# A 180-degree image rotation: 64 KB rows in one resident SBUF tile, with the first 16 images on partitions 32 to 95

## The chip, the cores and the metric

The kernel runs on one core of one Trainium2 chip. The time is device time in microseconds (us), the median of several executions. The profile is one execution; its span, from the first to the last instruction, is about 1.5 to 1.8 us shorter than the time. KB and MB of a transfer are powers of two in the text (4 MB is 4,194,304 bytes); GB/s is 10^9 bytes per second.

The five engines meet here as follows: VectorE (DVE in the profile) reverses data inside SBUF; the queues of SyncE (SPq) and ScalarE (ACTq) only issue DMA transfers. The transfers run on the core's 16 DMA engines, which both queues share (in the kernel before, the packets of the one queue took 48.9% of 16 engines' span and those of the other 48.0%).

## The reference

```python
def setup_inputs():
    batch, c, h, w = 32, 3, 256, 256
    return {"x": np.random.randn(batch, c, h, w).astype(np.float32)}

def reference(x):
    return np.rot90(x, k=2, axes=(-2, -1)).astype(np.float32)
```

A rotation by 180 degrees reverses each of the 96 images (32 x 3) of 65,536 floats (256 KB) end to end. So 25.17 million bytes are read, reversed, and 25.17 million written: 50.33 million bytes through the DMA engines.

## The kernel before

Three passes of 32 images. An image is cut into 8 rows of 32 KB; rows 0 to 3 of 32 images fill the 128 partitions of one tile, rows 7 to 4 those of another. VectorE reverses halves of a row, and each half goes out in rows of 16 KB. Two input buffers per tag and four output buffers let the queues run ahead.

```python
    for pp in range(n_pass):                     # 3 passes of NG = 32 images; Q = 4, S = 8
        nsl = slice(pp * NG, (pp + 1) * NG)
        tinF = tin_pool.tile([P, BLK], x.dtype, tag="F")      # 128 x 8192, bufs=2
        tinB = tin_pool.tile([P, BLK], x.dtype, tag="B")
        nc.sync.dma_start(out=tinF[:, :], in_=x3[nsl, 0:Q, :])
        nc.sync.dma_start(out=tinB[:, :], in_=x3[nsl, S - 1:Q - 1:-1, :])

        tF0 = tout_pool.tile([P, HB], x.dtype, tag="t")       # 128 x 4096, bufs=4
        nc.vector.tensor_copy(out=tF0[:, :], in_=tinB[:, 2 * HB - 1:HB - 1:-1])
        nc.scalar.dma_start(out=o4[nsl, 0:Q, 0, :], in_=tF0[:, :])
        # ... three more copies and stores of this form
```

## Time and profile before

| | before |
|---|---|
| time, median | 123.8 us |
| span of the profile | 122.3 us |
| VectorE busy | 27.2 us, 22% |
| data rate over the span | 412 GB/s |
| packets | 2592, of which 2304 carry data |

The page of the kernel before, cut to its main lines. The digits cut the span into 40 slices of 3.06 us; 9 means 90% busy or more. The two last lines are the DMA queues: packets, megabytes, and the share of 16 engines' span that their packets took.

```profile
span 122.3 us, 93 instructions
...
DVE  0000000399500000610160003307337156100000
...
DMA  5798989899999998999999999999999999999992
GB/s 171 343 472 386 472 386 482 375 482 359 348 450 407 466 429 386 472 423 397 439 455 413 477 434 391 413 429 434 429 434 434 439 429 434 429 439 434 429 429 113
DMA packets 2592, 50.33 MB, mean 412 GB/s; under 512 B 288, under 2 KB 288, under 8 KB 288
...
q1 hardware_dynamic: 864, 25.17, 48.9%
q10 hardware_dynamic: 1728, 25.17, 48.0%
```

VectorE idles most of the time while the DMA row has no hole between its ends, and the two queues together hold the 16 engines for 96.9% of the span. This kernel is bound by the DMA engines. Waits of VectorE cost nothing here, since transfers are always queued ahead: the DMA digits are 8 or 9 from the third slice to the last but one.

Rates by stretch, from the windows view of the same kernel (start:end, length, VectorE busy, GpSimd busy, clock, DMA share, GB/s):

```profile
core 0: us, DVE busy (x) POOL busy (x), PEclk, DMA share, GB/s
2.00:25.00 23.00, 1.65 (x1) 0.00 (x0) 1.00 1.02 429
27.00:33.00 6.00, 5.25 (x3) 0.00 (x0) 1.00 1.08 401
33.00:78.00 45.00, 6.88 (x3) 0.00 (x0) 1.00 0.99 427
78.00:120.00 42.00, 11.47 (x5) 0.00 (x0) 1.00 1.01 431
```

The rate is about 430 GB/s whether the engines only read (2 to 25, 429), mix (33 to 78, 427) or only write (78 to 120, 431). Only the stretch where the first stores come in is lower (27 to 33, 401).

The trace also records every packet; a row of a transfer is one packet (768 packets of 32 KB read, 1536 of 16 KB written). A 32 KB read packet takes 1213 ns at the median, a 16 KB write packet 611 ns.

### The profile page before, as it was taken

What the parts mean: (1) busy time and instruction counts of PE and PEld (TensorE: products, weight loads), DVE (VectorE), ACT (ScalarE), POOL (GpSimd) and SP (SyncE); (2) the same over time, 40 slices, a digit from 0 to 9 for tenths busy, and PEclk for the clock granted to TensorE, in tenths of its full rate; (3) what the DMA queues carried; (4) which work ended last, traced back from release to release, by engine and by line L of the source; (5) the groups of instructions that cost most, each with busy time, mean ns of one, the idle gap of its engine ahead of it and who ended that gap; (6) DMA issues with size and microseconds to landing.
All of it is one profiled execution on the core that took longest, in us unless ns stands there. A gap on an engine that the chain in (4) does not pass through costs nothing.

```text
span 122.3 us, 93 instructions
## 1 busy us (share of the span) xinstructions
DVE 27.2 (22%) x12; POOL 0.2 (0%) x4
## 2 busy tenths in 40 slices
DVE  0000000399500000610160003307337156100000
POOL 0000000000000000000000000000000000000000
DMA  5798989899999998999999999999999999999992
GB/s 171 343 472 386 472 386 482 375 482 359 348 450 407 466 429 386 472 423 397 439 455 413 477 434 391 413 429 434 429 434 434 439 429 434 429 439 434 429 429 113
DMA packets 2592, 50.33 MB, mean 412 GB/s; under 512 B 288, under 2 KB 288, under 8 KB 288
## 3 DMA queue, kind: packets, MB, share of 16 engines
q1 hardware_dynamic: 864, 25.17, 48.9%
q10 hardware_dynamic: 1728, 25.17, 48.0%
HBM read 25.17 MB, written 25.17 MB: 412 GB/s over the span
## 4 chain that ended last, share of the span: by engine, by line
DMA 69%; DVE 11%; another core or an unknown queue 4%; SPq 0%; issue 0%; DVEq 0%
DMA out_dram<-tF 37%; DMA tinB<-in_x_dram 18%; DMA out_dram<-tB 14%; DVE tB L64 4%; DVE tF L60 4%; DVE tF L52 2%; DVE tB L56 2%; SPq L48 0%; DVEq L64 0%; DVEq L60 0%
## 5 line engine op out<-in xcount | busy, mean ns | idle before, releaser
L52 DVE COPY tF<-tinB 128x4096 f32<-128x4096 f32 x3 | 6.9, 2294 | 43.8 <-DMA tinB<-in_x_dram 41.2
L60 DVE COPY tF<-tinB 128x4096 f32<-128x4096 f32 x3 | 6.9, 2291 | 14.7 <-DMA out_dram<-tF 14.7
L56 DVE COPY tB<-tinF 128x4096 f32<-128x4096 f32 x3 | 6.9, 2292 | 11.1 <-DMA out_dram<-tB 11.1
L64 DVE COPY tB<-tinF 128x4096 f32<-128x4096 f32 x3 | 6.9, 2291 | 7.6 <-DMA out_dram<-tB 7.6
L80 POOL MEMSET const-bfloat16-1.0<- 128x1 bf16 x1 | 0.1, 102 | 0.0
L80 POOL MEMSET const-uint8-127<- 128x1 uint8 x1 | 0.1, 102 | 0.0
L80 POOL MEMSET const-float32-0.0<- 128x1 f32 x1 | 0.1, 99 | 0.2 <-issue 0.2
L80 POOL MEMSET const-float32-1.0<- 128x1 f32 x1 | 0.1, 99 | 0.0
## 6 DMA issues: line engine op xcount, KB each, us to landing
tinF<-in_x_dram SPq DMA_DIRECT2D x3, 4096.0 KB, 32.2
tinB<-in_x_dram SPq DMA_DIRECT2D x3, 4096.0 KB, 32.9
out_dram<-tF ACTq DMA_DIRECT2D x6, 2048.0 KB, 20.0
out_dram<-tB ACTq DMA_DIRECT2D x6, 2048.0 KB, 23.1
```

Source lines behind the costliest of these rows:

```text
L52: nc.vector.tensor_copy(out=tF0[:, :], in_=tinB[:, 2 * HB - 1:HB - 1:-1])
L56: nc.vector.tensor_copy(out=tB0[:, :], in_=tinF[:, 2 * HB - 1:HB - 1:-1])
L60: nc.vector.tensor_copy(out=tF1[:, :], in_=tinB[:, HB - 1::-1])
L64: nc.vector.tensor_copy(out=tB1[:, :], in_=tinF[:, HB - 1::-1])
L80: nc = _bacc.Bacc("TRN2", target_bir_lowering=False, num_devices=1)
```

## The change

Its intent: fewer and larger packets (rows of 64 and 32 KB), one tile of three 64 KB slots per partition instead of many buffers, and a small first group of 16 images so that stores can start early. Those 16 images take 64 partitions, 32 to 95, filled by four transfers that each take every fourth partition. After that come two groups of 32 images on all 128 partitions and a last group of 16 images, which fills 128 partitions with half-size rows (8 rows of 32 KB per image).

```diff
-    NG = 32
-    ... 3 passes of 32 images, tiles of 32 KB in, 16 KB out
+    E = L // 4                      # 16384 floats: rows of 64 KB
+    K = E // 4                      # 4096: one copy
+    A0, B0, C0 = 0, E, 2 * E        # three slots
+    S = pool.tile([P, 3 * E], x.dtype, tag="S")
+
+    for q in range(4):
+        nc.sync.dma_start(out=S[32 + q:96:4, A0:A0 + E],
+                          in_=rows(xi, 0, 16, 4)[:, q, :])
+    nc.sync.dma_start(out=S[:, B0:B0 + E], in_=rows(xi, 16, 32, 4))
+    for p0 in (32, 64):
+        reverse(C0, A0, E, p0, p0 + 32)                  # 4 copies each
+    nc.scalar.dma_start(out=rows(oi, 0, 16, 4)[:, ::-1, :],
+                        in_=S[32:96, C0:C0 + E])         # first store
+
+    nc.sync.dma_start(out=S[:, A0:A0 + E], in_=rows(xi, 48, 32, 4))   # third load
+    reverse(C0, B0, E)
+    nc.scalar.dma_start(out=rows(oi, 16, 32, 4)[:, ::-1, :],
+                        in_=S[:, C0:C0 + E])             # second store
+
+    nc.sync.dma_start(out=S[:, B0:B0 + E // 2], in_=rows(xi, 80, 16, 8))   # fourth load
+    h = E // 2
+    o = rows(oi, 48, 32, 4)[:, ::-1, :]
+    reverse(B0 + h, A0 + h, h)
+    nc.scalar.dma_start(out=o[:, :, 0:h], in_=S[:, B0 + h:B0 + E])
+    reverse(C0, A0, h)
+    nc.scalar.dma_start(out=o[:, :, h:E], in_=S[:, C0:C0 + h])
+    reverse(A0 + h, B0, h)
+    nc.scalar.dma_start(out=rows(oi, 80, 16, 8)[:, ::-1, :],
+                        in_=S[:, A0 + h:A0 + E])         # last store, 16 x 8 rows
```

Here `rows(t, first, n, s)` views images `first` to `first+n-1` of `t` as `n` images of `s` rows, and `reverse(dst, src, size)` is `size/4096` copies on VectorE.

More of the change, by code (lines that the diff above doesn't have):

```diff
@@ L23 @@
     B, C, H, W = x.shape
-    N = B * C
     L = H * W
-    NG = 32
-    Q = P // NG
-    S = 2 * Q
-    BLK = L // S
-    HB = BLK // 2
-    x3 = x.rearrange("b c h w -> (b c) (h w)").rearrange(
-        "n (s e) -> n s e", s=S)
-    o4 = out.rearrange("b c h w -> (b c) (h w)").rearrange(
-        "n (s j f) -> n s j f", s=S, f=HB)
-    tin_pool = ctx.enter_context(tc.tile_pool(name="tin", bufs=2))
-    tout_pool = ctx.enter_context(tc.tile_pool(name="tout", bufs=4))
-    n_pass = N // NG
-    for pp in range(n_pass):
-        nsl = slice(pp * NG, (pp + 1) * NG)
-        tinF = tin_pool.tile([P, BLK], x.dtype, tag="F")
-        tinB = tin_pool.tile([P, BLK], x.dtype, tag="B")
-        nc.sync.dma_start(out=tinF[:, :], in_=x3[nsl, 0:Q, :])
-        nc.sync.dma_start(out=tinB[:, :], in_=x3[nsl, S - 1:Q - 1:-1, :])
-        tF0 = tout_pool.tile([P, HB], x.dtype, tag="t")
-        nc.vector.tensor_copy(out=tF0[:, :], in_=tinB[:, 2 * HB - 1:HB - 1:-1])
-        nc.scalar.dma_start(out=o4[nsl, 0:Q, 0, :], in_=tF0[:, :])
-        tB0 = tout_pool.tile([P, HB], x.dtype, tag="t")
-        nc.vector.tensor_copy(out=tB0[:, :], in_=tinF[:, 2 * HB - 1:HB - 1:-1])
-        nc.scalar.dma_start(out=o4[nsl, S - 1:Q - 1:-1, 0, :], in_=tB0[:, :])
-        tF1 = tout_pool.tile([P, HB], x.dtype, tag="t")
-        nc.vector.tensor_copy(out=tF1[:, :], in_=tinB[:, HB - 1::-1])
-        nc.scalar.dma_start(out=o4[nsl, 0:Q, 1, :], in_=tF1[:, :])
-        tB1 = tout_pool.tile([P, HB], x.dtype, tag="t")
-        nc.vector.tensor_copy(out=tB1[:, :], in_=tinF[:, HB - 1::-1])
-        nc.scalar.dma_start(out=o4[nsl, S - 1:Q - 1:-1, 1, :], in_=tB1[:, :])
@@ new lines, with rows, reverse @@
+    xi = x.rearrange("b c h w -> (b c) (h w)")
+    oi = out.rearrange("b c h w -> (b c) (h w)")
+    E = L // 4
+    K = E // 4
+    A0, B0, C0 = 0, E, 2 * E
+    pool = ctx.enter_context(tc.tile_pool(name="slots", bufs=1))
+    S = pool.tile([P, 3 * E], x.dtype, tag="S")
+    def rows(t, first, n, s):
+        return t[first:first + n, :].rearrange("n (s e) -> n s e", s=s)
+    def reverse(dst, src, size, p0=0, p1=P):
+        for c in range(0, size, K):
+            hi = src + size - c
+            lo = hi - K
+            nc.vector.tensor_copy(
+                out=S[p0:p1, dst + c:dst + c + K],
+                in_=S[p0:p1, hi - 1:(lo - 1 if lo else None):-1])
```

## The prediction

What is left of the layout step, 4 MB in 9.7 us, is the author's estimate: 4,194,304 bytes at the 433 GB/s of the undisturbed packets in the trace of the kernel before. The 2:1 sharing that step 2 speaks of can be counted in the same trace: from 34 to 78 us 384 read packets of 32 KB and 395 write packets of 16 KB start.

> **What bounds the kernel now.** The 16 DMA engines: the page's slices show DMA at 98-99% nearly throughout, its two queues 96.9% of 16 engines' span; DVE is 22% busy. Packet records: a 32 KB read takes 1211 ns undisturbed, a 16 KB write 611 ns, 48 and 96 per engine: 116.8 us, about 433 GB/s. [...] The rest of the 122.3 us span: first packet at 2.1, slow reads 1.6 (the first of each engine, and from 27 to 33 us as the first writes come in), 0.6 spread between engines, 1.2 from last packet to end. The measured time is 1.45 us above the span.
>
> **What the change does.**
> - *Bytes:* the same 50.33 MB.
> - *Packets:* 611 and 1211 ns imply 11 ns per packet beside the bytes. With 64 and 32 KB rows there are 20 + 8 reads and 12 + 24 writes per engine; at an estimated 2411 ns per 64 KB, 115.9 us. Gain 0.9 us.
> - *Layout:* partitions 32 to 95. [...] I expect full rate: 4 MB in 9.7 us.
> - *DVE:* 2.2 us per 4096-element copy whatever the partitions (assumed), so the first 16 images cost eight copies, 17.7 us. In total 18 copies, 40 us, still far under the DMA, but with three slots instead of six buffers they sit between transfers.
>
> **Where it lands** (433 GB/s, 2.2 us per copy, 0.4 us last packet to landing, 1.4 us issue to first packet, as at the start):
> 1. The first 4 MB lands at 13.3; eight copies end at 31.1; the second load (8 MB) leaves the engines at 31.8. The first write and the third load are issued only at 31.1, first packets 32.5: **gap 1, 0.7 us**.
> 2. They share the engines packet by packet (before: read and write shared 2:1, the ratio of packet sizes). The write ends after about 8 of 12 packet times; landing and spread 1.4, four copies 8.9, issue 1.5: 11.8 us against 9.7 us of reads left: **gap 2, 2.1 us**; none if the write goes first, 4.5 if the reads get one 64 KB packet ahead. Mean 1.8.
> 3. From there 24 MB are queued ahead of DVE; no gap.
>
> Sum: 2.1 + 115.9 + 1.6 + 0.6 + 1.2 = 121.4; with 2.5 of gaps 123.9 span, 125.3 time. The change looks tuned, so I shade down: **125.0 us**, range 122.6 to 127.4. Chances: faster by over 2% 0.06, within 2% 0.70, slower by over 2% 0.24.
>
> **What would show it.** DMA by slices: two dips, near 32 and 63 us, 98-99% elsewhere; about 1200 packets instead of 2592. Groups: 32-partition copies at 2.2-2.3 us each. Waits: DVE waiting about 20 us for the first write (31 to 53) and over 20 us for the second. Chain: first load, eight copies, first write, four copies, then DMA to the end. The last 58 us without a gap.
>
> **What would make it wrong.** Slower: reads running ahead of the first write in 64 KB packets; the strided or 64-partition transfers below 433 GB/s; a more ragged end between engines with large packets. Faster: the slow packets at the first writes vanish; copies of 32 partitions cheaper; shorter issue latency, closing both gaps (121.4 + 1.45 = 122.9).

## The result, and the profile after

The time rose from 123.8 to 140.87 us (four runs, 140.33 to 141.4), a ratio of 1.1383 (95% interval 1.1353 to 1.1413). Executions over 1.5% slower than the fastest of the same kernel are left out of the means. The ratios in this document are not quite the ratios of the medians. The output is right. The predicted 125.0 us and its range (122.6 to 127.4) were missed by far.

The page of the changed kernel, the same lines as before:

```profile
span 139.1 us, 86 instructions
...
DVE  0001999990000000089990000002993000000000
...
DMA  8697996968997896960298999996999999979981
GB/s 301 301 584 320 509 396 301 603 301 301 301 565 339 358 546 301 603 301 0 66 349 339 452 452 452 452 452 301 452 443 452 405 443 396 424 151 301 226 188 38
DMA packets 1216, 50.33 MB, mean 362 GB/s; under 512 B 192, under 2 KB 192, under 8 KB 192
...
q10 hardware_dynamic: 656, 25.17, 47.4%
q1 hardware_dynamic: 560, 25.17, 44.6%
```

There are two things to see. The DMA row has a hole (digits 0 and 2, near 66 us), which the kernel before nowhere has. And at the right end the DMA row is still full, but the GB/s row falls to about half. Busy engines that move half the bytes: that is a different loss from a hole, and the DMA share alone would not have shown it. (GB/s of single slices jump, because a packet is counted whole where it starts. The windows view counts in the same way.)

The windows view of the changed kernel puts numbers on it:

```profile
core 0: us, DVE busy (x) POOL busy (x), PEclk, DMA share, GB/s
2.00:31.00 29.00, 17.49 (x8) 0.00 (x0) 1.00 1.02 434
32.30:39.00 6.70, 0.00 (x0) 0.00 (x0) 1.00 0.99 323
39.00:63.00 24.00, 3.42 (x2) 0.00 (x0) 1.00 1.00 431
63.00:69.00 6.00, 6.00 (x4) 0.00 (x0) 1.00 0.00 0
69.50:77.00 7.50, 3.38 (x2) 0.00 (x0) 1.00 0.97 336
77.00:119.00 42.00, 8.99 (x4) 0.00 (x0) 1.00 1.01 436
119.00:137.00 18.00, 0.00 (x0) 0.00 (x0) 1.00 0.97 233
```

From 63 to 69 us no packet starts. The last packets before the hole end between 63.0 and 63.95, and the next start at 69.5, so an engine idles for 6.2 us on average. From 119 to 137 us the last store of 4 MB runs at 233 GB/s. The two stretches where loads and stores begin together (32 to 39 and 69.5 to 77) run at 323 and 336.

The timeline of the changed kernel (start, length, engine, line, what):

```profile
13.50 17.79 DVE L49 COPY S<-S 32x4096 f32<-32x4096 f32 x8 [13.50 <-DMA S<-in_x_dram]
31.32 0.33 SPq L67 DMA_DIRECT2D S<-in_x_dram  x1
31.32 0.66 ACTq L63 DMA_DIRECT2D out_dram<-S  x1
59.58 13.30 DVE L49 COPY S<-S 128x4096 f32<-128x4096 f32 x6 [28.28 <-DMA out_dram<-S]
68.50 0.33 SPq L73 DMA_DIRECT2D S<-in_x_dram  x1
68.51 0.59 ACTq L69 DMA_DIRECT2D out_dram<-S  x1
...
106.35 1.09 ACTq L83 DMA_DIRECT2D out_dram<-S  x1
```

The third load (L67) and the first store (L63) are issued at the same moment, 31.32. VectorE can go on only when that store has left slot C, at 59.58: 28.3 us for 4 MB. Its next copies end at 68.5, and only then are the next load (L73) and store (L69) issued. The third load had left the engines before 64.

The packet records, worked out per engine (sum over all packets of the time above the shortest packet of that kind and size, divided by 16) give the whole difference:

| us of an engine's time | before | after | difference |
|---|---|---|---|
| packets, undisturbed | 116.8 | 116.2 | -0.6 |
| slow packets of loads | 1.6 | 4.0 | +2.4 |
| slow packets of the last store | 0 | 7.8 | +7.8 |
| idle in the middle (near 32, 66 and 69 us) | 0 | 7.1 | +7.1 |
| start, uneven end, last landing | 3.9 | 4.0 | +0.1 |
| span | 122.3 | 139.1 | +16.8 |

(116.2 is 20 x 2.418 + 8 x 1.213 of reads and 12 x 2.418 + 24 x 1.213 of writes. The idle time was added up from the start and end of every packet. The fifth line is what is left of the span.)

### The profile page after: what moved, and what is told of

It is laid out like the page before. It is cut to its first block, busy times and chain, and to the rows that moved or that the text cites. A ratio compares the mean times of both kernels' runs of the same rounds, so it can differ in the third digit from the quotient of the medians.

```text
span 139.1 us, 86 instructions
## 1 busy us (share of the span) xinstructions
DVE 40.1 (29%) x18; POOL 0.2 (0%) x4
## 4 chain that ended last, share of the span: by engine, by line
DMA 51%; DVE 19%; issue 2%; DVEq 2%; SPq 1%
DMA out_dram<-S 44%; DVE S L49 19%; DMA S<-in_x_dram 8%; DVEq L110 2%; SPq L55 1%; DVEq L49 0%
## 5 line engine op out<-in xcount | busy, mean ns | idle before, releaser
L49 DVE COPY S<-S 128x4096 f32<-128x4096 f32 (+1 forms) x18 | 40.1, 2284 | 65.6 <-DMA S<-in_x_dram 37.0
```

The lines of the kernel that those rows point to most:

```text
L49: nc.vector.tensor_copy(out=S[p0:p1, dst + c:dst + c + K], in_=S[p0:p1, hi - 1:(lo - 1 if lo else None):-1])
```

## The experiments

The theories. **A**: the last store's shape, 16 images of 8 rows, decides which SBUF partitions are read at the same time, and some sets of partitions can be read or written at about half the rate only. This was conjecture: the trace names neither the engine nor the partition of a packet, so experiments 2 and 9 choose the partitions by hand. Rival **B**: the place of the last store, or its HBM addresses (16 images at a pitch of 256 KB), is slow. **C**: the hole comes from 64 KB load packets that run ahead of the first store and then share one to one with it. (In the changed kernel 32 load packets, two per engine on average, start between the first store's issue at 31.32 us and its first packet at 38.86; from 40 to 54 us 48 load packets and 47 store packets start.) Rivals **D** and **E**: it is only the length of the copies and the issue latencies, or a fixed wait of a store.

The first lot of experiments ran against 123.77 us of the kernel before (7 runs), the second against 123.63 (11 runs).

### 1. The same store addressed as 32 blocks of 4 rows

```diff
-    nc.scalar.dma_start(out=rows(oi, 80, 16, 8)[:, ::-1, :], ...
+    w = oi[80:96, :].rearrange("n (a s e) -> (n a) s e", a=2, s=4)
+    nc.scalar.dma_start(out=w[:, ::-1, :], in_=S[:, A0 + h:A0 + E])
```

> Wrong result on purpose: the last 4 MB store writes the same rows of SBUF into the same 4 MB of the output, addressed as 32 blocks of 4 rows instead of 16 images of 8 rows. Theory A [...]: its 32 KB packets fall from about 2.4 us to 1.21 us, the last store from 18.6 us to about 9.7, time 132 us (131 to 133.5). Rival B (the slowness belongs to the last store's place, its source columns or its region of HBM, not to the shape): no change, 140 to 141.5 us.

Measured: 132.65 us (132.24 to 133.19), ratio to before 1.0721. The packets of the last 4 MB fell from a median of 2438 ns to 1213 ns, none slower; from first to last packet they took 10.4 us instead of 18.6. The windows line of this kernel for its last store:

```profile
118.50:128.50 10.00, 0.00 (x0) 0.00 (x0) 1.00 0.97 419
```

So 8.2 us of the loss hang on the shape of the address alone: same bytes, same SBUF source, same 4 MB of HBM. Rival B falls as far as it speaks of place, columns or region. It could still be the order in which single engines touch HBM, if the shape changes that too (the trace does not show it); experiment 9 settles it.

### 2. The first 16 images on partitions 0 to 63

```diff
-        nc.sync.dma_start(out=S[32 + q:96:4, A0:A0 + E], ...
+        nc.sync.dma_start(out=S[q:64:4, A0:A0 + E], ...
-    for p0 in (32, 64):
+    for p0 in (0, 32):
-                        in_=S[32:96, C0:C0 + E])
+                        in_=S[0:64, C0:C0 + E])
```

> First 16 images on partitions 0 to 63 instead of 32 to 95; every HBM address, size, engine count and copy count stays. Theory A [...]: the 64 KB packets of the first four loads take about 4.9 us instead of 2.42, the first load lands near 23 us instead of 13.4, the first store is slowed too; time 150 to 162 us. Rival B (HBM addresses or pitch decide the packet time): packets stay at 2.42 us, time 140 to 141.5 us.

Measured: 153.06 us (152.59 to 153.72), ratio 1.2371. The first 64 load packets took 5082 ns at the median instead of 2418, and the first copy starts 10.4 us later than in the changed kernel (23.88 against 13.50). Windows line and timeline line of this kernel:

```profile
2.00:22.50 20.50, 0.00 (x0) 0.00 (x0) 1.00 1.07 237
...
23.88 17.79 DVE L49 COPY S<-S 32x4096 f32<-32x4096 f32 x8 [23.88 <-DMA S<-in_x_dram]
```

With HBM addresses unchanged, the partitions alone nearly halve the rate: 237 GB/s, where the changed kernel's four loads on partitions 32 to 95 take 2418 ns per 64 KB packet, or 434 GB/s on 16 engines. The engines are as busy as there (DMA share 1.07; in the changed kernel 1.02 from 2 to 31 us). So the choice of 32 to 95 in the change was right. Why partitions 0 to 63 are slow is not shown. One part of the expectation missed: the first store, now read from partitions 0 to 63, was not slowed (its 64 KB packets: 2418 ns at the median). It was issued together with the third load (41.71 and 41.70 us), while no store ran beside the slow loads; whether that spared it was not tested.

### 3. The third load behind the first store, on the same queue

```diff
-    nc.sync.dma_start(out=S[:, A0:A0 + E], in_=rows(xi, 48, 32, 4))
+    nc.scalar.dma_start(out=S[:, A0:A0 + E], in_=rows(xi, 48, 32, 4))
```

> The third load is issued on the store queue, behind the first store. Theory C (gap of 6.2 us near 66 us comes from two 64 KB read packets per engine running ahead of the first store, and then sharing one to one with it): first store packet about 1.2 us after its issue instead of 7.5, store lands near 44 us instead of 59.5, next issue near 52.5 while the third load still runs, no idle stretch in the middle; time 133 to 135.5 us. Rival D (the gap is the copies and issue latencies alone, which the order does not change): 139.5 to 141.5 us.

Measured: 133.25 us (133.21 to 133.42), ratio 1.0771. The first store's packets begin at 32.50, 1.3 us after its issue, instead of at 38.86, and the hole is gone. Windows line of this kernel where the changed one has its hole, then its timeline:

```profile
63.00:69.00 6.00, 1.88 (x1) 0.00 (x0) 1.00 1.01 350
...
31.17 0.67 ACTq L63 DMA_DIRECT2D out_dram<-S  x1
32.02 0.45 ACTq L67 DMA_DIRECT2D S<-in_x_dram  x1
43.80 8.90 DVE L49 COPY S<-S 128x4096 f32<-128x4096 f32 x4 [12.66 <-DMA out_dram<-S]
52.72 0.33 SPq L73 DMA_DIRECT2D S<-in_x_dram  x1
```

The copies still take 8.9 us, and the issues what they were (0.33 us on SPq and 0.59 on ACTq for the pair after these copies, in both kernels). Only the queue of the third load, and with it the order, changed: the store now goes ahead of the load, and slot C is free 11.3 us after the store's first packet instead of 20.7. VectorE gets slot C at 43.80 instead of 59.58, so the next transfers are queued while the third load still runs. Rival D falls.

### 4. The third load as two transfers of 32 KB half rows

```diff
-    nc.sync.dma_start(out=S[:, A0:A0 + E], in_=rows(xi, 48, 32, 4))
+    r3 = rows(xi, 48, 32, 4)
+    for c in (0, E // 2):
+        nc.sync.dma_start(out=S[:, A0 + c:A0 + c + E // 2],
+                          in_=r3[:, :, c:c + E // 2])
```

> The third load as two transfers of 32 KB half rows, on its own queue as before. Theory C: what runs ahead is two packets, so half the bytes, and the packet shares turn to 2:1 for the store: first store packet 3.5 to 4.5 us after issue instead of 7.5, store lands at 50 to 52 us instead of 59.5, gap near 66 us falls from 6.2 us to under 1; time 134 to 136 us. If a fixed wait of the store after an idle queue is the cause (rival E), the first store packet stays near 7.5 us and more than half of the gap remains: 137 us or more.

Measured: three runs took 136.24, 134.31 and 134.68 us, ratio 1.0914 (1.084 to 1.0988); a fourth, 142.03, was slow. The hole fell from 6.2 us of engine idleness to 0.1. VectorE got slot C at 52.92 instead of 59.58. (The slot was expected at 50 to 52.) A line of its timeline:

```profile
52.92 8.90 DVE L49 COPY S<-S 128x4096 f32<-128x4096 f32 x4 [21.82 <-DMA out_dram<-S]
```

But the first store packet came 6.3 us after its issue, not 3.5 to 4.5, and so nearer to rival E's 7.5. Between the issue and it, 48 load packets started, three per engine on average (in the changed kernel 32, two per engine), and these took 1.81 us each on average instead of 1.21. So "two packets run ahead" is not a rule; of 32 KB packets it was three, and they were slow. What helped was mostly the sharing of 64 KB to 32 KB per turn in favour of the store (that they take turns is the reading of the 48 load packets and 47 store packets counted above for the changed kernel): its packets took 13.8 us from first to last instead of 17.8, and the start gave 1.2. Rival E, a wait that every store has, falls by experiment 3, where the store began 1.3 us after its issue. What sets the length of the wait beside a load stays open: other stores waited 5.9 us (the second of the changed kernel, issued together with its fourth load) and 4.1 us (the first of the kernel before, issued while loads ran).

### 5. The kernel before with the packet sizes of the change

```diff
-        tinF, tinB: two loads of 4 MB, rows of 32 KB
+        tin = tin_pool.tile([P, BLK], x.dtype, tag="F")          # BLK = 16384, bufs=2
+        nc.sync.dma_start(out=tin[:, :], in_=x3[nsl, :, :])      # x3 with s=4
-        four stores per pass, rows of 16 KB, tout bufs=4
+        two stores per pass, rows of 32 KB (two copies each), tout bufs=2
```

> The kernel before with the packet sizes of the change alone: loads of 8 MB in rows of 64 KB into two buffers, stores in rows of 32 KB from two buffers, all transfers over 128 partitions with 32x4 stores. Theory: large packets are worth only their fixed cost, 24 x 2.418 + 48 x 1.213 = 116.3 us per engine against 116.8, and queued work leaves no gap: 122.8 to 124.0 us, within 1% of before. Rival (64 KB packets are harmful in themselves, through uneven engines or long slow phases when reads and writes meet): 125 us or more.

Measured: 123.26 us (122.68 to 123.38, 6 runs), ratio 0.9961 (0.9945 to 0.9977), with the right result. Large packets did no harm here, and they are worth 0.4%. This is the one version that beats both kernels, by an amount below 2%.

### 6. Experiments 1 and 3 together

> Both single repairs together (last store as 32 blocks of 4 rows, wrong result on purpose; third load behind the first store). If shape and order are separate causes they add: 140.9 - 8.2 - 7.6 = 125.1 us (124.3 to 126), and no idle stretch and no slow store remain. If one hides the other, 127 us or more.

Measured: 124.97 us (124.8 to 125.01), ratio 1.0107. The single gains are 8.2 and 7.6 us; 140.87 less both is 125.0. The engines' idle time in the middle is 0.6 us, without a hole near 66, and no packet of the last store took over 1213 ns. In the GB/s row of this kernel's page single slices jump, as above, but none falls to zero in the middle, and the end no longer runs at half:

```profile
GB/s 341 341 341 341 682 341 341 618 405 341 341 341 682 277 405 341 341 682 213 469 426 256 448 405 511 511 511 341 341 416 437 426 426 437 416 480 394 490 394 117
```

The two causes are separate and add up, and together they account for all but 1.3 us of the loss (124.97 against 123.63).

### 7. The reversal of the last 16 images' rows moved onto the load

```diff
-    nc.sync.dma_start(out=S[:, B0:B0 + E // 2], in_=rows(xi, 80, 16, 8))
+    nc.sync.dma_start(out=S[:, B0:B0 + E // 2], in_=rows(xi, 80, 16, 8)[:, ::-1, :])
-    nc.scalar.dma_start(out=rows(oi, 80, 16, 8)[:, ::-1, :],
+    nc.scalar.dma_start(out=rows(oi, 80, 16, 8),
```

> Right result: the order of the 8 rows of each of the last 16 images is reversed by the load, so the load has the 16x8 shape and the last store is 128 plain rows. Theory A [...]: last store back to 1.21 us per packet and about 9.7 us; the load's 32 KB read packets slow down instead, by an amount that is open, since its packets alternate with a store's: total 132 to 141 us. Rival B (place, columns or HBM region of the last store): the last store stays at 18.6 us and the load is unchanged, 140 to 141.5 us.

Measured: 139.49 us (138.07 to 140.05), ratio 1.1263, result right. The last store is a plain list of 128 rows now and back at 1213 ns per packet at the median. The fourth load had 1213 ns at the median in the changed kernel: it, too, is written `rows(..., 16, 8)` there, but without the reversal its rows follow one another through all 16 images, which makes it such a plain list. Reversed, it has 1982 ns. (Its packets share the engines with a store's: in the changed kernel 48 of this load's and 64 of the second store's start from 78 to 90 us.) Its completions on the 16 engines also spread over 4.2 us (from 100.9 to 105.1 us) instead of 0.9. The slowness moved with the shape, from a store to a load, and little was won. With this 16x8 shape, where the reversal is written decided which transfer paid, not whether one paid.

### 8. Both causes repaired, with the right result

The third load goes behind the first store as in experiment 3. The second store is cut in two halves, so that its slot is freed earlier. The last 16 images are held like the first 16:

```diff
-    nc.sync.dma_start(out=S[:, B0:B0 + E // 2], in_=rows(xi, 80, 16, 8))
+    for q in range(4):
+        nc.sync.dma_start(out=S[32 + q:96:4, B0:B0 + E],
+                          in_=rows(xi, 80, 16, 4)[:, q, :])
...
+    o3 = rows(oi, 80, 16, 4)[:, ::-1, :]
+    nc.scalar.dma_start(out=o3[:, :, 0:h], in_=S[32:96, A0 + h:A0 + E])
...
+    nc.scalar.dma_start(out=o3[:, :, h:E], in_=S[32:96, A0:A0 + h])
```

> Right result, both causes repaired: third load behind the first store; the last 16 images on partitions 32 to 95 in 64 KB rows like the first 16, stored as 16x4 in two halves; the second store in two halves so that its slot comes free earlier. Theories A and C: no store packet over 1.3 times its undisturbed time, no idle stretch over 1 us in the middle; 2.1 + 115.9 + 2.5 slow packets + 0.7 gap + 1.9 tail = 123.1 us span, 124.6 us time (123 to 126), that is level with before, since the change has only packet overhead to win. A result above 128 us would say that a third cause is left.

Measured: 124.88 us (124.79 to 125.08), ratio 1.0101 (1.0088 to 1.0114). The page of this kernel:

```profile
span 123.1 us, 99 instructions
...
DVE 53.6 (44%) x24; POOL 0.2 (0%) x4
...
DMA packets 1360, 50.33 MB, mean 409 GB/s; under 512 B 272, under 2 KB 272, under 8 KB 272
```

VectorE works twice as long as before (53.6 against 27.2 us) at little cost, since the DMA engines have no long hole. Slow packets are down to 2.5 us and idle time in the middle to 1.0. One part of the expectation missed: no store packet was to take over 1.3 times its undisturbed time, and packets of the first store took up to 3536 ns, 1.46 times 2418 (median 2444). The repaired design is 1.0% slower than the kernel before, clear of noise but below 2%. It does not beat it. It is also 1.6 us slower than experiment 5, which has the large packets without the three slots.

### 9a and 9b. The last store as explicit transfers of 16 rows

```diff
+    o8 = rows(oi, 80, 16, 8)[:, ::-1, :]
+    for j in range(8):
+        nc.scalar.dma_start(out=o8[:, j, :], in_=S[j:128:8, A0 + h:A0 + E])          # 9a
+        nc.scalar.dma_start(out=o8[:, j, :], in_=S[32 + j % 4:96:4, A0 + h:A0 + E])  # 9b instead
```

> Right result: the last store as 8 explicit transfers of 16 rows, transfer j taking partitions j, j+8, ... j+120, [...] Theory A: packets of the last 4 MB near 2.5 us, as in the changed kernel. If the 16x8 store is slow for another reason (its descriptors, its three-dimensional address), packets fall to 1.21 us.

> Wrong result on purpose: the same 8 transfers to the same HBM addresses, [...] but read from every fourth partition from 32 (twice over), [...]. Theory A: packets of the last 4 MB at 1.21 us. If HBM addresses (16 images at a pitch of 256 KB, rows of 32 KB) make the last store slow, they stay near 2.5 us.

Measured, one run each: 140.31 us for 9a and 132.23 us for 9b (before, on the same chip: 123.92). The packets of the last 4 MB took 2427 ns at the median in 9a and 1213 ns in 9b (126 of 128; none over 1231). The windows lines of the last store, 9a and then 9b:

```profile
120.00:136.00 16.00, 0.00 (x0) 0.00 (x0) 1.00 0.96 223
```

```profile
119.00:128.50 9.50, 0.00 (x0) 0.00 (x0) 1.00 1.00 428
```

Both runs write the same rows of HBM in the same order by the same eight transfers; only the SBUF partitions differ: every eighth together in 9a, which is the guess of what the 16x8 store reads together, and every fourth from 32 in 9b, as in the first loads. The packets carry this, not the two single times. Rival B, HBM addresses, falls. Every eighth partition reproduces the slow store of the change to about 11 ns of packet time, every fourth from 32 removes it. What stays inferred is that the single 16x8 transfer, too, is slow because of the partitions that are read together: the trace names neither the engine nor the partition of a packet. It fits all of 1, 7, 9a and 9b. One detail supports it. Taken in groups of 16 in the order of their starts, the last 128 packets of the changed kernel have 24 under 1360 ns: all of the first group and half of the fifth. In 9a, whose partitions are written out, there are 27: 13 in the first group and 8 in the fifth. Why the first and the fifth group escape the slowness was not tested.

## Why the prediction was wrong

- *The bound* was right: DMA engines at 433 GB/s, no byte removed, and 0.9 us (measured 0.6) to win from larger packets. Experiment 5 shows that this alone is worth 0.4%.
- *"From there 24 MB are queued ahead of DVE; no gap"*, with 433 GB/s for them: this is the step that failed. There was no gap, but the last 4 MB ran at 225 GB/s. The term that failed is the one rate for all packets: the prediction's sum gives each of the 24 writes of 32 KB per engine 1211 ns, and the last 8 took 2438 at the median, which costs 7.8 us. The list of what could go wrong named "the strided or 64-partition transfers", and those ran at full rate (the four strided loads and the 64-partition store of the changed kernel at 2418 ns per 64 KB packet at the median, 434 GB/s). The slow one was a transfer over all 128 partitions, whose 16x8 shape the prediction does not mention. Experiments 1, 7, 9a and 9b show that it behaves unlike a 32x4 store (2438 ns against 1213 per 32 KB packet in experiment 1).
- *Gap 2, "mean 1.8"*: the mechanism was right, the size was off. The prediction allowed for one 64 KB load packet ahead of the first store (4.5 us of gap); two got ahead, at 3.0 and 3.6 us on average instead of 2.4. The gap was 6.2 us. The prediction's list of what could go wrong had named this ("reads running ahead of the first write in 64 KB packets"). Together with gap 1 (0.7, as predicted) and a small one after it, idle time was 7.1 instead of 2.5.
- *Slow loads, "1.6"*: taken from before, where loads and stores met afresh once. In the change they meet afresh twice, and it measured 4.0.
- *Layout on partitions 32 to 95*: right in its result (2418 ns per 64 KB packet); its reason was not shown. A copy of 32 partitions takes as long as one of 128 (eight in 17.79 us, six in 13.30, 2.2 each): right. First landing (13.3), end of the eight copies (31.1) and gap 1 were met within 0.3 us.
- The sum: 15.2 us of span were missing (139.1 - 123.9). The last store accounts for 7.8 of them, the idle time for 4.6 and the slow loads for 2.4; the other 0.4 are packets (116.2 instead of 115.9) and ends.
- *"The change looks tuned, so I shade down"* was no measurement and should have had no weight. The chance of 0.24 for "slower" was too small: the range ended 2.1 us above the prediction's own sum of 125.3, which left room for a longer gap and none for a slow transfer.

## What to carry to other kernels

Where DMA engines are full, look at GB/s beside the busy share: a transfer over 128 partitions can hold all 16 engines (DMA share 0.97 here) and still move half the bytes (233 GB/s against 436 just before). Here its address shape did it, most likely through the partitions that are read together (experiments 9a and 9b, 2427 ns against 1213 per packet, show that these alone can do it; the mechanism behind that was not shown); groups of four partitions per outer index (32x4, 1213 ns) were safe here, and groups of eight (16x8, 2438 ns) were not. When a store frees the slot that the next work needs, try to issue it ahead of a competing large load, on the same queue if need be: here that brought its first packet from 7.5 us after the issue to 1.3. Fewer, larger packets alone were worth about their fixed cost, 0.4% here; with three slots in place of separate buffers even the repaired kernel stayed 1.0% behind.
